# Differential attention: scores of three maps in one PSUM tile of five banks, queries split once, norms for two heads at a time

## The chip, the core and the metric

The kernel runs on one core of a Trainium2 chip. TensorE (PE, with its weight loads PEld) multiplies, VectorE (DVE), ScalarE (ACT) and GpSimd (POOL) do the rest, and SyncE (SP) issues the transfers. Sums of matmuls land in PSUM, which has eight banks of 512 float32 columns in each of 128 partitions. The metric is the device time of one execution in microseconds (us).

## What is computed

Two layers of a backbone over 512 latent tokens and 256 context tokens, 1024 wide. In each layer a modulated norm feeds one input projection, whose columns go to a gated MLP over chunks, to a differential attention and to a convolution module; one output projection (`w_out`) and a gated residual follow, and then a gated feed-forward part. The change is in the attention:

```
def diff_attn(q, k, v, lam):
    s = jnp.einsum("bqhmd,bkhmd->bhmqk", q, k) * (B_QK_DIM ** -0.5)
    p = jax.nn.softmax(s, axis=-1)
    a = p[:, :, 0] - lam * p[:, :, 1]
    return jnp.einsum("bhqk,bkhd->bqhd", a, v)
...
o = blocked_diff_attn(q, k_all, v_all, lam)        # 4 heads, 2 softmax maps per head
yb = rms_norm(o, P["subln_g"]) * (1.0 - lam_init)  # norm over the 128 columns of a head
```

Latent queries see 768 keys (512 latent, 256 context); context queries see the 256 context keys, in layer 0 only.

## The kernel before

**Units.** Queries are taken in pairs of tiles: `pairs` lists (head, p) with p = 0, 1 for two halves of the latent tokens and p = 2 for the context, which comes first and in layer 0 alone. So layer 0 has 12 pairs and layer 1 has 8. Each pair is two units of 128 queries, and each unit has two maps. I call the units of a pair A and B, and their maps a0, a1, b0, b1. Over both layers there are 64 maps of 768 keys and 16 of 256 keys.

**A unit.** `scores` (L801 to L819) does for each map: matmuls of the high part (L812) and the low part (L813) of the queries with the keys `kk` into `pss`, the negated maximum over the keys on VectorE (`mx`, L815), and the exp on ScalarE (`e`), which reads `pss` again and sums into `sm`. `combine` (L820 to L833) makes the factor `cc` on VectorE, adds the two maps into one (`e`, L831) and keeps a diagonal tile `dg` on POOL, for the norm's small term. `transp` transposes the result in blocks of 128 keys on TensorE (`pat`, L113) and copies it to `ath`. `attn_v` (L853) multiplies with the values (`po`, L860), a float32 matmul in two passes, for both units of a pair; `subln` (L868) does the norm with a matmul against ones (`pr`), Ln and Exp, and splits the result into `yBh` and `yBl`.

**Queries.** `q_prep` (L776) transposes a pair's queries (`pq`). For the first pair of a layer ScalarE copies the high part to `qh`, twice, since a map's 64 rows are wanted in both halves of the partitions; for the others it goes through `qn`, with copies by ScalarE and POOL. VectorE subtracts for the low part into `qlz`, whose other half is zero.

**PSUM.** `pss` has two buffers of two banks, tag "w" (`pq`, `pat`, `po`, `pr`) three buffers of one bank, tag "f" one bank.

**Fill.** A part of the output projection, which needs no attention result (`wout` with part 0, tile `wo`, tag "f"), is written out behind the unit loop (L906 to L911): two slices in layer 0, three in layer 1. In layer 0 one group of it stands ahead of the loop.

**Order.** The text of the loop is not the order on the engines. A list scheduler sets it from priorities and from when buffers come free, with `scores` and `q_prep` a little ahead (SCP), and each engine then works through its own list, waiting on semaphores. A tile is what the scheduler tracks: it places a wait on the engine that last used the tile's buffer.

Of the kernel before, what the change touches and what calls it, by code (L numbers as in the profile page):

```python
# [9 lines left out]
F32 = mybir.dt.float32  # L10
F32R = mybir.dt.float32r
# [5 lines left out]
P = 128  # L17
# [27 lines left out]

FB, WB, EB, QB = 1, 3, 5, 3
MRB, MRW, RAWB, NSQ, NTB, KXB, FTB = 4, 2, 3, 2, 3, 3, 2

HP, SCP, RSP = 1000, 2, 60
# [29 lines left out]
def tile_backbone(  # L81
# [27 lines left out]
    def sub_lo(o, a, hi, eng=None):  # L109
        (eng or V).tensor_sub(o, a, hi.bitcast(F32))  # L110
# [211 lines left out]
    for l in range(DEPTH):  # L322
# [433 lines left out]
        with ExitStack() as ph:  # L756
# [5 lines left out]
            qlz = [sp.tile([P, 2, 256], F32R, name=f"qlz{x}") for x in range(2)]  # L762
            zero = sp.tile([P, 256], F32, name="zero")
            G.memset(zero, 0.0)
            for x in qlz:
                for m in range(2):
                    ms = slice((1 - m) * QKD, (2 - m) * QKD)
                    G.tensor_copy(x[ms, m], zero[ms])
            pairs = [(h, p) for p in range(2) for h in range(HEADS)]
            if not last:  # L770
                pairs = [(h, 2) for h in range(HEADS)] + pairs
            units = [(n, i) for n in range(len(pairs)) for i in range(2)]
            st = {}

            def q_prep(n):
                h, p = pairs[n]  # L776
                qh = sp.tile([P, 2, 256], F32R, tag="qh", name="qh", bufs=QB)
                ql = qlz[n % 2]
                pq = ps.tile([P, 256], F32, tag="w", name="pq", bufs=WB)
                for i in range(2):  # L780
                    T.transpose(pq[:, i * P:(i + 1) * P], qt[2 * p + i][:, h * P:(h + 1) * P], ident)
                if n == 0:
                    for m in range(2):
                        for a in range(2):
                            S.copy(qh[a * QKD:(a + 1) * QKD, m], pq[m * QKD:(m + 1) * QKD])
                    for m in range(2):
                        ms = slice(m * QKD, (m + 1) * QKD)
                        sub_lo(ql[ms, m], pq[ms], qh[ms, m])
                else:
                    qn = sp.tile([P, 256], F32R, tag="qn", name="qn", bufs=2)  # L790
                    S.copy(qn, pq)
                    for m in range(2):
                        src = qn[m * QKD:(m + 1) * QKD]
                        for a in range(2):
                            (G.tensor_copy if a else S.copy)(qh[a * QKD:(a + 1) * QKD, m], src)
                    for m in range(2):
                        ms = slice(m * QKD, (m + 1) * QKD)
                        sub_lo(ql[ms, m], pq[ms], qn[ms])
                st["q", n] = (qh, ql)

            def scores(n, i):  # L801
                h, p = pairs[n]
                k0, nk = (0, 6) if p < 2 else (LAT, 2)
                qh, ql = st["q", n]
                e = []
                sm = sp.tile([P, 2], F32, tag="sm", name="sm", bufs=4)
                for m in range(2):
                    pss = ps.tile([P, 1024], F32, tag="s", name="pss", bufs=2)
                    for (a, b) in ([(0, 512), (512, 768)] if p < 2 else [(0, 256)]):
                        ksl = slice(k0 + a, k0 + b)  # L810
                        qs = slice(i * P, (i + 1) * P)
                        T.matmul(pss[:, a:b], qh[:, m, qs], kk[:, 2 * h + m, ksl], start=True, stop=False)  # L812
                        T.matmul(pss[:, a:b], ql[:, m, qs], kk[:, 2 * h + m, ksl], start=False, stop=True)  # L813
                    mx = sp.tile([P, 1], F32, tag="mx", name="mx", bufs=4)
                    V.tensor_reduce(out=mx, in_=pss[:, :nk * P], op=ALU.max, axis=AX.X, negate=True)  # L815
                    em = sp.tile([P, TOK], F32, tag="e", name="e", bufs=EB)
                    act(em[:, :nk * P], pss[:, :nk * P], AF.Exp, bias=mx, accum_out=sm[:, m:m + 1])
                    e.append(em)
                st[n, i] = (e, sm)  # L819

            def combine(n, i):
                nk = 6 if pairs[n][1] < 2 else 2
                e, sm = st[n, i]
                cc = sp.tile([P, 1], F32, tag="cc", name="cc", bufs=4)
                if i == 0:
                    st["dg", n] = sp.tile([P, 2, P], F32, tag="dg", name="dg", bufs=3)
                dg = st["dg", n][:, i]
                V.reciprocal(out=cc, in_=sm[:, 1:2])
                V.scalar_tensor_tensor(out=cc, in0=cc, scalar=nlam, in1=sm[:, 0:1], op0=ALU.mult, op1=ALU.mult)
                e0, e1 = e[0][:, :nk * P], e[1][:, :nk * P]  # L830
                V.scalar_tensor_tensor(out=e0, in0=e1, scalar=cc, in1=e0, op0=ALU.mult, op1=ALU.add)  # L831
                G.tensor_scalar(out=dg, in0=epsi, scalar1=sm[:, 0:1], scalar2=sm[:, 0:1], op0=ALU.mult, op1=ALU.mult)
                st[n, i] = e[0]  # L833

            def transp(n, i):
                nk = 6 if pairs[n][1] < 2 else 2
                e = st[n, i]
                if i == 0:
# [12 lines left out]

            def attn_v(n):
                h, p = pairs[n]  # L853
                k0, nk = (0, 6) if p < 2 else (LAT, 2)
                at = st[n]
                po = ps.tile([P, 256], F32, tag="w", name="po", bufs=WB)
                hs = slice(h * P, (h + 1) * P)
                for c in range(nk):
                    kt = k0 // P + c
                    T.matmul(po, vt[:, kt, hs], at[:, c], start=c == 0, stop=c == nk - 1)  # L860
                o = sp.tile([P, 256], F32, tag="o", name="o", bufs=2)
                sq = sp.tile([P, 256], F32, tag="osq", name="osq", bufs=2)
                S.copy(o, po)
                S.activation(sq, o, AF.Square)
                G.tensor_add(sq, sq, st["dg", n].rearrange("p a q -> p (a q)"))
                st["sub", n] = (o, sq)

            def subln(n):  # L868
                h, p = pairs[n]
                o, sq = st["sub", n]  # L870
# [5 lines left out]
                ts = slice(p * 256, p * 256 + 256)  # L876
                S.copy(yBh[:, h, ts], o)
                sub_lo(yBl[:, h, ts], o, yBh[:, h, ts])

            first = [(g, i) for g in whole for i in range(2)]  # L880
            if l == 0:
                w0 = wout_w(0, (0,), "pool")
                g, i = first.pop(0)
                wout(0, (0,), w0, [g], ps, "f", FB, (i,))
            q_prep(0)
            nu = len(units)
            for u in range(nu + 8):
# [12 lines left out]
                if 0 <= v < nu and units[v][1] == 1:  # L900
                    attn_v(units[v][0])
                v = u - LAG[2]
                if 0 <= v < nu and units[v][1] == 1:
                    subln(units[v][0])

            for mp2 in range(NFILL[l]):  # L906
                if mp2 == 0 and l == 0:
                    for g, i in first:
                        wout(0, (0,), w0, [g], ps, "f", FB, (i,))
                else:  # L910
                    wout(mp2, (0,), wout_w(mp2, (0,), "pool"), whole, ps, "f", FB)  # L911
        kvs.close()


# [253 lines left out]
```

## Time and profile before

| | before |
|---|---|
| three runs | 1617.92, 1620.43, 1620.6 us, median 1620.43 |
| the profiled execution, its own time | 1616.07 us |
| span in the trace | 1614.0 us |
| TensorE busy | 1570.6 us (97%) |
| VectorE, ScalarE, POOL busy | 1020.4, 646.9, 105.9 us |
| mean granted clock of TensorE | 0.994 |

The span is the time from the first to the last recorded instruction of the profiled execution. Busy times are sums over each engine; TensorE's is modelled, since its matmuls overlap. Start times below are us from the span's start, and clock 1.00 is TensorE's level of 2.4 GHz.

### The profile page before, as it was taken

The numbers are of one execution on the slowest core, as the hardware profiler recorded it, in microseconds if no ns is written. First come the engines' busy times: TensorE is split into PE (matmuls) and PEld (weight loads), VectorE is DVE, ScalarE is ACT, GpSimd is POOL, SyncE is SP. The second block draws the span as 40 slices with busy tenths as digits, with TensorE's granted clock in tenths as the row PEclk, the third lists the DMA queues.
The fourth block names the chain that finished last, engine by engine and source line by source line (L and its number), as shares of the span: only waits on it lengthen the run. The fifth ranks groups of instructions, "written<-read, shape, count | busy, mean of one in ns | idle before, by whom it ended". The sixth has DMA issues, their size and how long they took to land.

```text
span 1614.0 us, 21207 instructions
## 1 busy us (share of the span) xinstructions
PE 1570.6 (97%) x8186; PEld 1292.4 (80%) x8186; DVE 1020.4 (63%) x1722; ACT 646.9 (40%) x1122; POOL 105.9 (7%) x126
## 2 busy tenths in 40 slices
PE   6999998999999999999999999999999999999999
PEld 4875776778888887878888887887778788888888
DVE  4497878969999983345544244896976544334433
ACT  5431568753532322234433133254764333123321
POOL 1130125310000000000000000000220000000000
PEclk9999999999999999999999999999999999999999
DMA  7625110015255888988611235653022322332232
GB/s 282 212 76 180 56 64 15 14 51 185 85 190 194 285 279 265 289 284 298 207 66 50 60 127 186 205 170 105 27 80 78 104 92 88 95 104 92 92 105 92
DMA packets 83140, 222.93 MB, mean 138 GB/s; under 512 B 12256, under 2 KB 14560, under 8 KB 82912
## 3 DMA queue, kind: packets, MB, share of 16 engines
q1 hardware_dynamic: 83040, 221.59, 41.6%
q8 instruction: 64, 1.05, 0.3%
q14 instruction: 36, 0.29, 0.1%
HBM read 190.10 MB, written 31.46 MB: 137 GB/s over the span
## 4 chain that ended last, share of the span: by engine, by line
PE 77%; DMA 10%; DVE 6%; ACT 4%; issue 2%; SPq 0%; POOL 0%; POOLq 0%; DVEq 0%; ACTq 0%
PE pp L267 10%; PE pp L266 10%; PE pp L268 10%; PE acc L433 5%; PE acc L441 5%; PE acc L434 5%; PE pd L268 4%; PE pd L267 4%; PE pd L266 4%; DMA in<-araw 3%; DMA araw<-in_w_in_dram 3%; PE po L860 3%; PE wo L266 2%; DMA mraw<-in_w_modT_dram 2%; PE wo L267 2%; PE wo L268 2%
## 5 line engine op out<-in xcount | busy, mean ns | idle before, releaser
L268 PE MATMUL pp<-hhi,wlo 128*128 128x512 f32 (+1 forms) x1072 | 380.0, 355 | 4.4 <-DVE wlo L110 4.4
L266 PE MATMUL pp<-hhi,whi 128*128 128x512 f32 (+1 forms) x1072 | 380.6, 356 | 1.7 <-ACT whi L224 1.4
L267 PE MATMUL pp<-hlo,whi 128*128 128x512 f32 (+1 forms) x1072 | 381.4, 356 | 0.8 <-DVE hlo L306 0.8
L224 ACT CAST whi<-raw 128x1024 fp32r<-128x1024 f32 (+1 forms) x167 | 170.9, 1025 | 389.9 <-PE pp L267 203.0
L110 DVE TENSOR_TENSOR wlo<-raw,whi 128x1024 fp32r<-128x1024 f32 (+2 forms) x154 | 185.4, 1206 | 218.4 <-ACT whi L224 211.1
L268 PEld LDWEIGHTS pp<-hhi,wlo 128*128 128x128 f32 x1072 | 202.3, 189 | 36.1 <-DVE wlo L110 5.2
L266 PEld LDWEIGHTS pp<-hhi,whi 128*128 128x128 f32 x1072 | 202.0, 189 | 36.0 <-ACT whi L224 3.3
L267 PEld LDWEIGHTS pp<-hlo,whi 128*128 128x128 f32 x1072 | 202.0, 189 | 32.8 <-DVE hlo L306 1.5
L266 PE MATMUL pd<-gh,whi 128*128 128x512 f32 (+1 forms) x550 | 192.9, 351 | 2.5 <-ACT whi L224 2.5
L268 PE MATMUL pd<-gh,wlo 128*128 128x512 f32 (+1 forms) x550 | 193.6, 352 | 0.8 <-DVE wlo L110 0.8
L267 PE MATMUL pd<-gl,whi 128*128 128x512 f32 (+1 forms) x550 | 193.1, 351 | 0.0
L266 PEld LDWEIGHTS pd<-gh,whi 128*128 128x128 f32 x550 | 103.8, 189 | 18.0 <-ACT whi L224 2.9
L268 PEld LDWEIGHTS pd<-gh,wlo 128*128 128x128 f32 x550 | 104.1, 189 | 15.7 <-DVE wlo L110 1.0
L267 PEld LDWEIGHTS pd<-gl,whi 128*128 128x128 f32 x550 | 103.9, 189 | 15.1
L691 DVE SCALAR_TENSOR_TENSOR cacc<-cin,cw,cacc 128x783 f32<-128x783 f32 (+1 forms) x120 | 103.4, 916 | 3.4 <-ACT cacc L686 3.4
L110 DVE TENSOR_TENSOR araw<-araw,ahi 128x512 f32<-128x512 f32 x56 | 38.5, 691 | 93.3 <-ACT ahi L248 93.2
L1027 DVE TENSOR_TENSOR ft<-ft,pp 128x256 f32<-128x256 f32 (+1 forms) x66 | 39.1, 598 | 74.4 <-PE pp L268 66.7
L196 DVE CUSTOM_DVE_ANT_0 mraw<-mraw,csil,bmod 128x1024 f32<-128x1024 f32 x64 | 81.7, 1279 | 5.9 <-DMA mraw<-in_w_modT_dram 5.5
L248 ACT CAST ahi<-araw 128x512 fp32r<-128x512 f32 x56 | 34.7, 620 | 121.5 <-DMA araw<-in_w_in_dram 83.7
L433 PE MATMUL acc<-whi,hhi 128*128 128x512 f32 x192 | 77.8, 405 | 0.0
L434 PE MATMUL acc<-whi,hlo 128*128 128x512 f32 x192 | 76.9, 401 | 0.0
L101 ACT ACTIVATE ft<-ft 128x768 f32<-128x768 f32 (+1 forms) x44 | 32.6, 740 | 103.2 <-DVE ft L1022 103.2
(224 smaller groups left out, 2599.3 us busy)
## 6 DMA issues: line engine op xcount, KB each, us to landing
raw<-in_w_gv_dram SPq DMA_DIRECT2D x88, 512.0 KB, 3.3
mraw<-in_w_modT_dram SPq DMA_DIRECT2D x64, 512.0 KB, 4.3
raw<-in_w_down_dram SPq DMA_DIRECT2D x34, 512.0 KB, 3.6
wh<-in SPq DMA_DIRECT2D x24, 512.0 KB, 4.4
wl<-in SPq DMA_DIRECT2D x24, 512.0 KB, 4.5
raw<-in_w_in_dram SPq DMA_DIRECT2D x20, 512.0 KB, 4.1
araw<-in_w_in_dram SPq DMA_DIRECT2D x40, 256.0 KB, 3.6
in<-ahi SPq DMA_DIRECT2D x40, 256.0 KB, 4.7
```

What stands on the lines that cost most here:

```text
L110: (eng or V).tensor_sub(o, a, hi.bitcast(F32))
L196: r = V.tensor_tensor_reduce(out=junk, in0=w, in1=csil[:, s], scale=1.0, scalar=bmod[:, l, i, f:f + 1], op0=ALU.mult, op1=ALU.add, accum_o ...
L224: S.copy(hi, raw)
L266: T.matmul(o, lhi, rhi, start=start, stop=False)
L267: T.matmul(o, lhi, rlo, start=False, stop=False)
L268: T.matmul(o, llo, rhi, start=False, stop=stop)
L433: T.matmul(pt[t], hhi[hs], wh[:, a], start=k2 + a == 0, stop=False)
L434: T.matmul(pt[t], hlo[hs], wh[:, a], start=False, stop=False)
L441: T.matmul(pt[t], hhi[hs], wl[:, a], start=False, stop=k2 + 1 == KD // 2 and a == 1)
L691: V.scalar_tensor_tensor(out=cacc[:, c, :cn], in0=cin[:, c, j:j + cn], scalar=cw[:, l, c, j:j + 1], in1=cacc[:, c, :cn], op0=ALU.mult, op1 ...
L860: T.matmul(po, vt[:, kt, hs], at[:, c], start=c == 0, stop=c == nk - 1)
L1027: V.tensor_mul(t[:, a:b], t[:, a:b], pp[s][1][:, :b - a])
```

## The change

All maps go into one tile `sbank` of five banks. The map with the number nmap takes the 768 columns that start at 0, 768 or 1536 in turn; its matmuls are cut where a bank ends. The tag "f" is gone: the fill uses tag "w", as `pq`, `pat`, `po` and `pr` do. The queries are split once into `qn` (high and low part, 128 rows each), and four transfers on SP's queue (64x2x256 values each) put them into both halves of `qq`. The norm handles two heads: one Square, one Ln, one Exp and one write of `yBh` and `yBl` for two, and the term `dg` comes in by a matmul of its own (L862) in place of an addition on POOL. In `transp` the second copy of unit B moves from VectorE to ScalarE, and `dg` has five buffers.

```diff
-FB, WB, EB, QB = 1, 3, 5, 3
+WB, EB, QB = 3, 5, 3
...
+            sbank = ps.tile([P, 5 * 512], F32, name="sbank")
+            nmap = [0]
...
-                qh = sp.tile([P, 2, 256], F32R, tag="qh", name="qh", bufs=QB)
-                ql = qlz[n % 2]
+                qq = sp.tile([P, 2, 2, 256], F32R, tag="qq", name="qq", bufs=QB)
+                qn = sp.tile([P, 2, 256], F32R, tag="qn", name="qn", bufs=2)
                 pq = ps.tile([P, 256], F32, tag="w", name="pq", bufs=WB)
...
-                    S.copy(qn, pq)
-                    for m in range(2):
-                        src = qn[m * QKD:(m + 1) * QKD]
-                        for a in range(2):
-                            (G.tensor_copy if a else S.copy)(qh[a * QKD:(a + 1) * QKD, m], src)
-                    for m in range(2):
-                        ms = slice(m * QKD, (m + 1) * QKD)
-                        sub_lo(ql[ms, m], pq[ms], qn[ms])
-                st["q", n] = (qh, ql)
+                S.copy(qn[:, 0], pq)
+                sub_lo(qn[:, 1], pq, qn[:, 0])
+                for m in range(2):
+                    for a in range(2):
+                        nc.sync.dma_start(out=qq[a * QKD:(a + 1) * QKD, :, m].bitcast(F32), in_=qn[m * QKD:(m + 1) * QKD].bitcast(F32))
+                st["q", n] = (qq[:, 0], qq[:, 1])
...
-                    pss = ps.tile([P, 1024], F32, tag="s", name="pss", bufs=2)
-                    for (a, b) in ([(0, 512), (512, 768)] if p < 2 else [(0, 256)]):
+                    x0 = nmap[0] % 3 * TOK
+                    nmap[0] += 1
+                    pss = sbank[:, x0:x0 + TOK]
+                    cut = 256 if x0 % 512 else 512
+                    for (a, b) in ([(0, cut), (cut, TOK)] if p < 2 else [(0, 256)]):
...
-                    if c0 == 0:
+                    if c0 == 0 or i == 1:
                         S.copy(at[osl], pat[:, :cn_])
...
-                G.tensor_add(sq, sq, st["dg", n].rearrange("p a q -> p (a q)"))
...
-                pr = ps.tile([P, 256], F32, tag="w", name="pr", bufs=WB)
-                T.matmul(pr, ones, sq, start=True, stop=True)
+                pr = ps.tile([P, 2, 256], F32, tag="w", name="pr", bufs=WB)
+                for y in range(2):
+                    T.matmul(pr[:, y], ones, sq[:, y], start=True, stop=False)
+                    T.matmul(pr[:, y], ones, st["dg", 2 * x + y].rearrange("p a q -> p (a q)"), start=False, stop=True)
...
-                wout(0, (0,), w0, [g], ps, "f", FB, (i,))
+                wout(0, (0,), w0, [g], ps, "w", WB, (i,))
...
-                if 0 <= v < nu and units[v][1] == 1:
-                    subln(units[v][0])
+                if 0 <= v < nu and units[v][1] == 1 and units[v][0] % 2 == 1:
+                    subln(units[v][0] // 2)
```

How this stands on the engines is shown at three places. First TensorE in layer 1, before, where a pair is well under way: two maps have a tile `pss` each, `pat` of another unit and the fill `wo` stand between their matmuls.

```order
L113 MATMUL pat_10001<-ident_62,e_9922 128x128 [waits DVE_49]
L812 MATMUL pss_9985<-kk_9207,qh_9902 128x512 [waits Activation_49,Pool_49]
L113 MATMUL pat_10001<-ident_62,e_9922 128x128
L813 MATMUL pss_9985<-kk_9207,qlz1_9885 128x512
L113 MATMUL pat_10001<-ident_62,e_9922 128x128
L812 MATMUL pss_9985<-kk_9207,qh_9902 128x256
L113 MATMUL pat_10001<-ident_62,e_9922 128x128
L813 MATMUL pss_9985<-kk_9207,qlz1_9885 128x256
L113 MATMUL pat_10007<-ident_62,e_9922 128x128 x2
L266 MATMUL wo_10716<-yACh_8637,wh_10698 128x512
L267 MATMUL wo_10716<-yACl_8638,wh_10698 128x512
L268 MATMUL wo_10716<-yACh_8637,wl_10700 128x512
```

The same part of the program after: all maps write `sbank`, `pat` and `po` stand between two maps, and no `wo` is there.

```order
L113 MATMUL pat_9945<-ident_62,e_9851 128x128 [waits DVE_49,PE_49]
L113 MATMUL pat_9945<-ident_62,e_9851 128x128 x3
L113 MATMUL pat_9951<-ident_62,e_9851 128x128 [waits PE_49]
L113 MATMUL pat_9951<-ident_62,e_9851 128x128
L848 MATMUL po_9955<-ath_9867,vt_9089 128x256 [waits PE_49]
L848 MATMUL po_9955<-ath_9867,vt_9089 128x256 x3
L800 MATMUL sbank_9765<-kk_9088,qq_9777 128x256 [waits Activation_49]
L801 MATMUL sbank_9765<-kk_9088,qq_9777 128x256
L800 MATMUL sbank_9765<-kk_9088,qq_9777 128x512
L801 MATMUL sbank_9765<-kk_9088,qq_9777 128x512
L848 MATMUL po_9955<-ath_9867,vt_9089 128x256 x2
L800 MATMUL sbank_9765<-kk_9088,qq_9833 128x512 [waits DMAHW7_49,DMAHW6_49,Activation_49]
```

The transposes, which trailed the maps by several, stand right behind one map each, and the fill has left this place.

Second, ScalarE in layer 1 before: `e` are the exps of the maps, in the order of the maps.

```order
L101 ACTIVATE e_9947,sm_9939<-pss_9940,mx_9945 128x768
L101 ACTIVATE e_9956,sm_9939<-pss_9949,mx_9954 128x768
L101 ACTIVATE e_9983,sm_9975<-pss_9976,mx_9981 128x768
L848 COPY ath_10000<-pat_10001 128x4x128
L101 ACTIVATE e_9992,sm_9975<-pss_9985,mx_9990 128x768
L848 COPY ath_10000<-pat_10035 128x4x128
L101 ACTIVATE e_10019,sm_10011<-pss_10012,mx_10017 128x768
L101 ACTIVATE e_10028,sm_10011<-pss_10021,mx_10026 128x768
L791 CAST qn_10049<-pq_10046 128x256
```

And after, over one pair:

```order
L101 ACTIVATE e_9859,sm_9844<-sbank_9765,mx_9857 128x768
L836 COPY ath_9944<-pat_9945 128x4x128
L101 ACTIVATE e_9885,sm_9878<-sbank_9765,mx_9883 128x768
L851 COPY o_9962<-po_9955 128x256
L101 ACTIVATE e_9893,sm_9878<-sbank_9765,mx_9891 128x768
L836 COPY ath_9944<-pat_9986 128x4x128
L101 ACTIVATE e_9928,sm_9921<-sbank_9765,mx_9926 128x768
L836 COPY ath_9944<-pat_9992 128x2x128
L779 CAST qn_9997<-pq_9998 128x256
L101 ACTIVATE e_9936,sm_9921<-sbank_9765,mx_9934 128x768
```

Two exps that stood together are now parted by copies of `ath`, `o` and `qn`, which wait for TensorE.

Third, TensorE at the end of layer 1's attention before: `pr` are the sums of the norms, `wo` the fill.

```order
L860 MATMUL po<-ath,vt 128x256 x6
L872 MATMUL pr<-osq,ones 128x256
L113 MATMUL pat<-ident,e 128x128 x6
L266 MATMUL wo<-yACh,wh 128x512
L267 MATMUL wo<-yACl,wh 128x512
L268 MATMUL wo<-yACh,wl 128x512
L860 MATMUL po<-ath,vt 128x256 x6
L872 MATMUL pr<-osq,ones 128x256
L266 MATMUL wo<-yACh,wh 128x512
L267 MATMUL wo<-yACl,wh 128x512
L268 MATMUL wo<-yACh,wl 128x512
L266 MATMUL wo<-yACh,wh 128x512
```

And after:

```order
L113 MATMUL pat<-ident,e 128x128 x6
L848 MATMUL po<-ath,vt 128x256 x6
L861 MATMUL pr<-osq,ones 128x256
L862 MATMUL pr<-dg,ones 128x256
L861 MATMUL pr<-osq,ones 128x256
L862 MATMUL pr<-dg,ones 128x256
L266 MATMUL wo<-yACh,wh 128x512
L267 MATMUL wo<-yACl,wh 128x512
L268 MATMUL wo<-yACh,wl 128x512
```

All of the fill of this layer stands behind the last `pr`; layer 0 reads likewise.

## Rows read from the trace of the kernel before

**Rows 1.** Timeline of TensorE, first and next matmul of both stages: start, us, instruction

```profile
244.22 0.82 PE L781 MATMUL pq<-ident,q 128*128 128x128 f32 x6
...
349.49 0.58 PE L267 MATMUL wo<-yACl,whi 128*128 128x512 f32 x1
...
1121.80 0.81 PE L781 MATMUL pq<-ident,q 128*128 128x128 f32 x6
...
1123.01 0.50 PE L812 MATMUL pss<-kk,qh 128*128 128x512 f32 x1
...
1204.68 0.58 PE L267 MATMUL wo<-yACl,wh 128*128 128x512 f32 x1
```

**Rows 2.** Windows 245-300, 300-349, 1123-1160, 1160-1205: their sum, busy us by engine

```profile
sum 186.00, PE 172.34 PEld 140.12 DVE 159.83 ACT 139.72 POOL 60.14; mean PE 43.08 PEld 35.03 DVE 39.96 ACT 34.93 POOL 15.04
```

**Rows 3.** Waits, 245 to 349: us in total, times, longest us

```profile
PE pss L812 <- ACT e L101: 6.3, 9, 1.1
```

**Rows 4.** Timeline of all engines, 277 to 281 us

```profile
277.27 0.85 PE L113 MATMUL pat<-ident,e 128*128 128x128 f32 x6 [0.24 <-ACT osq L101]
...
277.94 0.58 ACT L848 COPY ath<-pat 128x512 f32<-128x512 f32 x1 [0.73 <-PE pat L113]
...
278.42 0.91 ACT L101 ACTIVATE e<-pss,mx 128x768 f32<-128x768 f32 x1
...
279.45 0.16 DVE L828 RECIPROCAL cc<-sm 128x1 f32<-128x1 f32 x1 [0.19 <-ACT e L101]
...
279.47 0.50 PE L812 MATMUL pss<-kk,qh 128*128 128x512 f32 x1 [1.13 <-ACT e L101]
...
279.60 0.38 ACT L791 CAST qn<-pq 128x256 fp32r<-128x256 f32 x1
...
279.98 0.42 DVE L110 TENSOR_TENSOR yBl<-o,yBh 128x256 fp32r<-128x256 f32 x1
...
280.16 0.28 PE L813 MATMUL pss<-kk,qlz 128*128 128x256 f32 x1
```

**Rows 5.** Timeline, layer 1, scores and the maximum behind them

```profile
1144.20 0.28 PE L813 MATMUL pss<-kk,qlz 128*128 128x256 f32 x1
...
1144.52 0.96 DVE L815 TENSOR_REDUCE mx<-pss 128x1 f32<-128x768 f32 x1 [0.27 <-PE pss L813]
```

**Rows 6.** Timeline, layer 0, a map of 256 keys

```profile
248.47 0.39 PE L812 MATMUL pss<-kk,qh 128*128 128x256 f32 x1 [0.79 <-ACT e L101]
...
248.69 0.28 PE L813 MATMUL pss<-kk,qlz 128*128 128x256 f32 x1
...
249.15 0.42 DVE L815 TENSOR_REDUCE mx<-pss 128x1 f32<-128x256 f32 x1
...
249.61 0.47 ACT L101 ACTIVATE e<-pss,mx 128x256 f32<-128x256 f32 x1 [0.32 <-DVE mx L815]
```

**Rows 7.** Groups by line and shape, 1123 to 1205: busy us, mean ns

```profile
L831 DVE SCALAR_TENSOR_TENSOR e<-e,cc 128x768 f32<-128x768 f32 x16 | 16.2, 1010 | 0.1
```

**Rows 8.** Timeline of TensorE, layers 0 and 1

```profile
340.00 2.86 PE L860 MATMUL po<-ath,vt 128*128 128x256 f32 x12
...
1146.14 0.39 PE L267 MATMUL wo<-yACl,wh 128*128 128x512 f32 x1
1146.37 0.40 PE L268 MATMUL wo<-yACh,wl 128*128 128x512 f32 x1
```

**Rows 9.** Windows: length, busy by engine, granted clock, DMA share, GB/s

```profile
248.00:250.00 2.00, 0.96 (x4) 0.59 (x4) 1.88 (x8) 1.66 (x7) 1.44 (x4) 1.00 0.08 33
252.00:254.00 2.00, 2.00 (x8) 1.61 (x8) 1.63 (x7) 0.76 (x3) 0.44 (x1) 0.50 0.00 0
276.00:280.00 4.00, 2.62 (x16) 2.06 (x15) 3.81 (x9) 3.23 (x9) 1.54 (x2) 1.00 0.00 0
```

**Rows 10.** DMA issues: count, KB each, median us to landing

```profile
out_dram<-xT SPq DMA_DIRECT2D x4, 128.0 KB, 1.8
...
gbase<-in_qk_g_dram SPq DMA_DIRECT2D x2, 128.0 KB, 3.7
```

More of the change, by code (lines that the diff above doesn't have):

```diff
@@ L760, in tile_backbone @@
             V.tensor_scalar_mul(gsub, sublt[:, l:l + 1], 1.0 - lam0)
[L762 to L765, printed above, removed]
-                for m in range(2):
-                    ms = slice((1 - m) * QKD, (2 - m) * QKD)
-                    G.tensor_copy(x[ms, m], zero[ms])
             pairs = [(h, p) for p in range(2) for h in range(HEADS)]
@@ L781, in q_prep @@
                     T.transpose(pq[:, i * P:(i + 1) * P], qt[2 * p + i][:, h * P:(h + 1) * P], ident)
-                if n == 0:
-                    for m in range(2):
-                        for a in range(2):
-                            S.copy(qh[a * QKD:(a + 1) * QKD, m], pq[m * QKD:(m + 1) * QKD])
-                    for m in range(2):
-                        ms = slice(m * QKD, (m + 1) * QKD)
-                        sub_lo(ql[ms, m], pq[ms], qh[ms, m])
-                else:
-                    qn = sp.tile([P, 256], F32R, tag="qn", name="qn", bufs=2)
-                    S.copy(qn, pq)
-                    for m in range(2):
-                        src = qn[m * QKD:(m + 1) * QKD]
-                        for a in range(2):
-                            (G.tensor_copy if a else S.copy)(qh[a * QKD:(a + 1) * QKD, m], src)
-                    for m in range(2):
-                        ms = slice(m * QKD, (m + 1) * QKD)
-                        sub_lo(ql[ms, m], pq[ms], qn[ms])
-                st["q", n] = (qh, ql)
+                S.copy(qn[:, 0], pq)
[4 more added lines that the diff above has]
+                st["q", n] = (qq[:, 0], qq[:, 1])
             def scores(n, i):
@@ L825, in combine @@
                 if i == 0:
-                    st["dg", n] = sp.tile([P, 2, P], F32, tag="dg", name="dg", bufs=3)
+                    st["dg", n] = sp.tile([P, 2, P], F32, tag="dg", name="dg", bufs=5)
                 dg = st["dg", n][:, i]
@@ L860, in attn_v, with subln @@
                     T.matmul(po, vt[:, kt, hs], at[:, c], start=c == 0, stop=c == nk - 1)
-                o = sp.tile([P, 256], F32, tag="o", name="o", bufs=2)
-                sq = sp.tile([P, 256], F32, tag="osq", name="osq", bufs=2)
-                S.copy(o, po)
-                S.activation(sq, o, AF.Square)
-                G.tensor_add(sq, sq, st["dg", n].rearrange("p a q -> p (a q)"))
[L866 to L870, printed above, removed]
-                pr = ps.tile([P, 256], F32, tag="w", name="pr", bufs=WB)
-                T.matmul(pr, ones, sq, start=True, stop=True)
+                if n % 2 == 0:
+                    st["sub", n // 2] = sp.tile([P, 2, 256], F32, tag="o", name="o", bufs=2)
+                S.copy(st["sub", n // 2][:, n % 2], po)
+            def subln(x):
+                h, p = pairs[2 * x]
+                o = st["sub", x]
+                sq = sp.tile([P, 2, 256], F32, tag="osq", name="osq", bufs=2)
+                S.activation(sq, o, AF.Square)
+                pr = ps.tile([P, 2, 256], F32, tag="w", name="pr", bufs=WB)
+                for y in range(2):
+                    T.matmul(pr[:, y], ones, sq[:, y], start=True, stop=False)
+                    T.matmul(pr[:, y], ones, st["dg", 2 * x + y].rearrange("p a q -> p (a q)"), start=False, stop=True)
                 act(sq, pr, AF.Ln, scale=1.0 / P)
@@ L875, in subln @@
                 V.scalar_tensor_tensor(out=o, in0=o, scalar=gsub, in1=sq, op0=ALU.mult, op1=ALU.mult)
-                ts = slice(p * 256, p * 256 + 256)
-                S.copy(yBh[:, h, ts], o)
-                sub_lo(yBl[:, h, ts], o, yBh[:, h, ts])
+                osl = (slice(None), slice(h, h + 2), slice(p * 256, p * 256 + 256))
+                S.copy(yBh[osl], o)
+                sub_lo(yBl[osl], o, yBh[osl])
             first = [(g, i) for g in whole for i in range(2)]
@@ L908, in tile_backbone @@
                     for g, i in first:
-                        wout(0, (0,), w0, [g], ps, "f", FB, (i,))
+                        wout(0, (0,), w0, [g], ps, "w", WB, (i,))
                 else:
-                    wout(mp2, (0,), wout_w(mp2, (0,), "pool"), whole, ps, "f", FB)
+                    wout(mp2, (0,), wout_w(mp2, (0,), "pool"), whole, ps, "w", WB)
         kvs.close()
```

## Prediction

> **What bounds the kernel now.** I read the page first, then the busy time of the attention stages by windows, then the waits there, then the timeline around single maps. Attention runs twice. In layer 0 TensorE starts it with `pq` at 244.22, and the matmul behind the last `pr` starts at 349.49; in layer 1 the same two stand at 1121.80 and 1204.68 [rows 1]. In these stretches TensorE is busy for 172.3 of 186.0 us, VectorE 159.8, ScalarE 139.7 [rows 2]. The reader is to see three engines that are nearly full at once: TensorE has the end, and 13.7 us is all that its idle time could give back. Its wait for ScalarE's exp `e` is 6.3 us in nine places [rows 3]: with two buffers a map waits for the exp of the map two before, which is mostly over. What keeps TensorE full is that the `wout` fill, `pat` and `po` stand between the maps.
>
> **The new order of maps.** The two listings of TensorE show what the program text hides. `sbank` is one tile, and the first matmul of each map waits for ScalarE; counted through ScalarE's order, the count it asks for is that of the exp of the map directly ahead, whichever columns that one read. So there is not a depth of three but of one: scores, maximum, exp, and only then the next scores.
>
> One link, from single rows. Exp ends at 278.42+0.91 = 279.33 and the scores start at 279.47: 0.14. They end at 280.16+0.28: 0.97 for four matmuls [rows 4]. From their end to the maximum is 1144.52-1144.48 = 0.04, the maximum takes 0.96 [rows 5]; in the 256-key map it ends at 249.57 and the exp starts at 249.61: 0.04 [rows 6]. The exp takes 0.91 [rows 4]. Together 3.03 us for a map of 768 keys. For 256 keys: 0.14, scores 248.47 to 248.97 = 0.50, 0.04, 0.42, 0.04, 0.47 [rows 6], together 1.61. There are 64 large maps (8 pairs x 4 in each layer) and 16 small ones: 64x3.03 + 16x1.61 = 219.7 us of bare chain, while both stages now take 105.3 + 82.9 with everything in them. This alone puts the kernel behind.
>
> **What else stands in the chain.** The listings of TensorE and ScalarE put other work into it. A walk through one large pair, from the end of the exp of its map a1 at 0: next scores 0.14 to 1.11. VectorE meanwhile has reciprocal (0.12 after the exp's end, 0.16 long [rows 4]), `cc` and the long combination (start at 0.58, 1.01 long [rows 7]); it stands before the maximum of b0, which so runs 1.59 to 2.54. `pat` starts behind the combination at 1.70, its first copy 0.67 later, 0.58 long [rows 4], and that copy stands before exp(b0): 2.95 to 3.85 in place of 2.13 to 3.03. Four `po` matmuls stand before the scores of b1: each is two passes, and twelve passes last 2.86, the last some 0.4 of it [rows 8], so 0.22 each: eight take 1.75 and end at 4.15, 0.16 after the exp's hand-over; `po` again 0.88, the copy `o` before exp(b1), which ends at 7.42. The second half goes likewise, with `qn` (0.38) and the low half (0.42) [rows 4] before the last maximum: the pair ends at 14.4, and with `pr` on TensorE in every second pair 14.5. Bare chain: 12.1. The same walk with the small rows gives 8.2 for a small pair (bare 6.4).
>
> **Clock.** TensorE would be busy some 60% of this. At 0.96 of 2 us in 248 to 250 the granted clock was still full, and in 252 to 254 it was 0.50 (1.2 GHz); at 2.62 of 4 in 276 to 280 it was 1.00 [rows 9]. The large pairs lie near the latter, the small ones near the former. At the 1.2 GHz level the scores of a pair cost 3.9 more (2.0 for small maps): 18.4 and 10.2. I take a fifth of that way for the large pairs, 15.3, and half of it for the small, 9.2; the ends stay for the range.
> The Trainium skill's page "TensorE: Matmul & The Clock Gate", section "A second HAM failure mode: psum-queue depth-cycling", says that short idle times between groups of matmuls can make the clock go back and forth between its levels. By that rule the sum would be that of the second rival; the row at 276 to 280 speaks against it at the large maps, the one at 252 to 254 for it.
>
> **Fill.** It now takes tag `w` and stands behind the last `pr` in both layers. A 512-wide matmul starts 0.23 after the last [rows 8], a 256-wide one at half. Layer 0: 48 wide and 36 narrow = 15.4, of which all but 1.8 lie inside the stage now; layer 1: 72 wide = 16.7, all but 1.2 inside. In before they cover waits; now nothing runs beside them but the end of the norms.
>
> **Start.** `pq` to first scores is 1123.01-1121.80 = 1.2 now [rows 1]. After: `pq` 0.25, `qn` 0.38, low half 0.42, then DMAs. Their landing is not in the trace for this size from SBUF; the nearest rows, 128 KB each, land in 1.8 and 3.7 [rows 10]. With two issues ahead and hand-overs, 3.6 to 5.8; I take 4.8, and no fill stands beside it. For later pairs `pq` stands some five maps (15 us) ahead, which hides the DMAs; without that cover each pair would pay about 4.
>
> **End.** Behind the last exp: combination to 1.6, `pat` and copies to 3.0, `po` 2.6, copy, Square and four `pr` 2.8 and hand-overs, 8.7; less 0.9 that the walk counts already: 7.8.
>
> **At nothing.** Fewer qh copies, one low half in place of two, no zeroing, no POOL sum, norms of two heads in one instruction, one copy moved to ScalarE: VectorE, ScalarE and POOL then wait for the chain, so what is saved lies in their idle time. `dg` in `pr` adds 40 passes of some 0.22 [rows 8], 8.8 us of TensorE, covered by the exps; if the cover were gone, 8.8 is its price. SP's queue has the q DMAs behind weight loads that are early.
>
> **Sum.** Layer 0: 4.8 + 4x9.2 + 8x15.3 + 7.8 + 15.4 = 187.2. Layer 1: 4.8 + 122.4 + 7.8 + 16.7 = 151.7. Together 338.9. Before: 105.3+1.8 and 82.9+1.2 = 191.2. More by 147.7: on the profiled execution's 1616.1 it makes 1763.8. The median of the runs, 1620.4, lies 4.4 above that execution: **1768**.
>
> **Rivals.**
> 1. *The bare chain.* Everything but scores, maximum and exp fits into gaps: 219.7 + 2x(4.8+7.8) + 32.1 = 277.0, more by 85.8: 1706. For it: much of the walk's extra is hand-over that I estimated. Against: ScalarE's order has the copies before the exps.
> 2. *The 1.2 GHz level throughout.* 4x10.2 + 16x18.4 + 25.2 + 32.1 = 392.5, more by 201.3: 1822. For it the row of 252 to 254, against it that of 276 to 280.
> 3. *Other side: maps wait by bank.* If a map waited only for readers of its own banks, two maps in a row wait for each other (they share a bank) and the third is free: three maps in two links, 2.02 us per map, against some 2.6 now (82.9 us for 32 maps). The chain would not bind; the 13.7 us of idle could go and 8.8 of `dg` come: 4.9 less, 1616. It decides for faster as long as the uncovered start costs less than 4.9 us in all; if start and end are uncovered twice, it turns to about +20 (1640). Against it: the counts of the waits, which are those of the map ahead for free columns too.
> The Trainium skill's page "PSUM — Partial Sum Buffer", section "PSUM bank collisions raise a hardware error", has the rule to guard by bank and quadrant, not by address; by it, this third case would be allowed. No row of the kernel before has one tile over five banks, so none shows how it is guarded.
>
> **Numbers.** The forecast 0.62; rival 1 0.13; rival 2 0.15; rival 3 on the slow side 0.06; rival 3 faster 0.02, and its two effects cancelling 0.02. Between the bare chain and the low clock lies nine tenths: 1706 to 1822. A measurement tells about 0.2% from no change: faster 0.02, same 0.02, slower 0.96.
>
> **What would show it.** Right: in both attention stages TensorE's largest wait is `sbank` for `e`, once per map, starts of maps lie 3.0 to 4.5 us apart; the stages last near 170 and 135 us without the fill; `wo` runs alone behind `pr`; VectorE's time per map is unchanged. The clock there tells the forecast from rival 2, and the time between an exp's end and the maximum of the next map tells it from rival 1. Wrong: scores that run beside the exp of the map ahead.

## The result, and the profile after

| | before | after |
|---|---|---|
| median of the runs | 1619.37 us (1617.92 to 1620.6, 4 runs) | 1768.67 us (1766.87 to 1772.21, 4 runs) |
| profiled execution, its span | 1614.0 us | 1770.4 us |
| mean granted clock | 0.994 | 0.954 |

The ratio is 1.0927, 95% interval 1.091 to 1.0944: slower by 9.3%, 149.3 us. The forecast was 1768, with 1706 to 1822.

The page of the changed kernel, first the busy times, then TensorE's busy tenths and granted clock in 40 slices of 44 us:

```profile
PE 1632.5 (92%) x8226; PEld 1335.2 (75%) x8226; DVE 1011.7 (57%) x1666; ACT 633.9 (36%) x1056; POOL 62.8 (4%) x60
...
PE   7999976768999999998999999996669999999998
...
PEclk8999986889999999999999999996889999999999
```

The same two rows of the kernel before:

```profile
PE   6999998999999999999999999999999999999999
PEclk9999999999999999999999999999999999999999
```

After, there are two dents, slices 6 to 10 (in the clock row 6 to 9) and 28 to 30. They lie in the two attention stages; elsewhere the rows differ from those of before by a tenth in single slices.

The stages' ends on TensorE, from the timeline of the changed kernel:

```profile
244.23 1.18 PE L778 MATMUL pq<-ident,q 128*128 128x128 f32 x6
250.18 0.55 PE L800 MATMUL sbank<-kk,qq 128*128 128x256 f32 x1 [4.76 <-DMA qq<-qn]
...
415.66 0.59 PE L862 MATMUL pr<-dg,ones 128*128 128x256 f32 x2
...
1205.04 0.82 PE L778 MATMUL pq<-ident,q 128*128 128x128 f32 x6
...
1210.12 0.77 PE L800 MATMUL sbank<-kk,qq 128*128 128x512 f32 x1 [4.26 <-DMA qq<-qn]
...
1344.05 0.59 PE L862 MATMUL pr<-dg,ones 128*128 128x256 f32 x2
```

From `pq` to the end of the last `pr` layer 0 takes 172.0 us and layer 1 139.6. Read the same way, before takes 105.6 and 83.2 (the 105.3 and 82.9 of [rows 1] end where the matmul behind the last `pr` starts), with nearly all of the fill inside; after, none of it is inside. The waits of the changed kernel over the whole span (us in total, times, longest):

```profile
DVE mx L803 <- PE sbank L801: 85.1, 55, 5.2
PE sbank L800 <- ACT e L101: 74.1, 48, 2.5
```

The wait for exp was 6.3 us before, over the whole span too, all of it in layer 0 [rows 3]; now it is 74.1, at 48 of the 80 maps. And the maximum waits for the scores, 55 times: each engine waits for the one ahead in the chain. One half of a large pair in layer 1, with the exp of map a1 first:

```profile
1248.65 0.90 ACT L101 ACTIVATE e<-sbank,mx 128x768 f32<-128x768 f32 x1 [1.58 <-DVE mx L803]
...
1249.69 0.58 PE L800 MATMUL sbank<-kk,qq 128*128 128x256 f32 x1 [2.13 <-ACT e L101]
...
1250.12 1.02 DVE L819 SCALAR_TENSOR_TENSOR e<-e,cc 128x768 f32<-128x768 f32 x1
...
1250.71 0.63 PE L801 MATMUL sbank<-kk,qq 128*128 128x512 f32 x1
1251.38 0.96 DVE L803 TENSOR_REDUCE mx<-sbank 128x1 f32<-128x768 f32 x1 [0.24 <-PE sbank L801]
...
1252.41 0.58 ACT L836 COPY ath<-pat 128x512 f32<-128x512 f32 x1 [2.77 <-PE pat L113]
1252.60 1.95 PE L848 MATMUL po<-ath,vt 128*128 128x256 f32 x8
...
1252.89 0.91 ACT L101 ACTIVATE e<-sbank,mx 128x768 f32<-128x768 f32 x1
...
1254.19 0.59 PE L800 MATMUL sbank<-kk,qq 128*128 128x512 f32 x1
...
1255.35 0.96 DVE L803 TENSOR_REDUCE mx<-sbank 128x1 f32<-128x768 f32 x1 [2.09 <-PE sbank L801]
1256.15 0.37 ACT L851 COPY o<-po 128x256 f32<-128x256 f32 x1 [2.26 <-PE po L848]
1256.41 0.91 ACT L101 ACTIVATE e<-sbank,mx 128x768 f32<-128x768 f32 x1
...
1257.46 0.50 PE L800 MATMUL sbank<-kk,qq 128*128 128x512 f32 x1 [1.35 <-ACT e L101]
...
1257.90 1.02 DVE L819 SCALAR_TENSOR_TENSOR e<-e,cc 128x768 f32<-128x768 f32 x1
...
1258.15 0.28 PE L801 MATMUL sbank<-kk,qq 128*128 128x256 f32 x1
1258.84 0.95 DVE L803 TENSOR_REDUCE mx<-sbank 128x1 f32<-128x768 f32 x1
```

The scores of b0 start at 1249.69, 0.14 after the exp's end, though they write other columns than that exp read. The copy `ath` (1252.41) stands ahead of exp(b0) at 1252.89; `po`, from 1252.60, stands ahead of the scores of b1 at 1254.19; the copy `o` ahead of exp(b1). These are the walk's steps in its order, but for one: here it is not the combination (1250.12 to 1251.14) that holds the maximum of b0 back. The scores themselves end only at 1251.34, after 1.65 us in place of 0.97, and the maximum starts 0.04 later; over 1249.6 to 1251.4 the granted clock was 0.50, the 1.2 GHz level. In the next half the scores take 0.97 (1257.46 to 1258.43, with a clock of 0.93 over 1257.4 to 1259.9), and there the combination, 1257.90 to 1258.92, does hold the maximum back.

For comparison, the next map in layer 1 before, behind the scores that end at 1144.48 [rows 5]:

```profile
1144.35 0.48 PE L812 MATMUL pss<-kk,qh 128*128 128x512 f32 x1
...
1146.03 0.91 ACT L101 ACTIVATE e<-pss,mx 128x768 f32<-128x768 f32 x1
```

Its scores start 1.7 us ahead of the exp of the map before it.

### The profile page after: what moved, and what is told of

It is laid out like the page before. It is cut to its first block, busy times and chain, and to the rows that moved or that the text cites. A ratio compares the mean times of both kernels' runs of the same rounds, so it can differ in the third digit from the quotient of the medians.

```text
span 1770.4 us, 21260 instructions
## 1 busy us (share of the span) xinstructions
PE 1632.5 (92%) x8226; PEld 1335.2 (75%) x8226; DVE 1011.7 (57%) x1666; ACT 633.9 (36%) x1056; POOL 62.8 (4%) x60
## 4 chain that ended last, share of the span: by engine, by line
PE 46%; DMA 7%; ACT 2%; DVE 2%; issue 1%; SPq 0%; ACTq 0%; DVEq 0%
PE pp L267 6%; PE pp L268 6%; PE pp L266 6%; PE pd L268 4%; PE pd L267 4%; PE pd L266 4%; PE acc L433 2%; PE acc L441 2%; PE acc L434 2%; DMA in<-araw 2%; DMA araw<-in_w_in_dram 2%; DMA araw<-in_w_out_dram 2%; PE po L848 1%; ACT e L101 1%; PE sbank L800 1%; PE pat L113 1%
## 5 line engine op out<-in xcount | busy, mean ns | idle before, releaser
L800 PE MATMUL sbank<-kk,qq 128*128 128x256 f32 (+1 forms) x144 | 70.3, 492 | 83.1 <-ACT e L101 74.1
L803 DVE TENSOR_REDUCE mx<-sbank 128x1 f32<-128x768 f32 (+1 forms) x80 | 68.0, 850 | 85.4 <-PE sbank L801 85.1
L800 PEld LDWEIGHTS sbank<-kk,qq 128*128 128x128 f32 x144 | 34.6, 240 | 103.1 <-ACT e L101 90.2
L101 ACT ACTIVATE e<-sbank,mx 128x768 f32<-128x768 f32 (+1 forms) x80 | 65.5, 818 | 51.5 <-DVE mx L803 51.0
```

Of the source, the lines that this page charges most:

```text
L101: r = S.activation(out, in_, func, **kw)
```

## Experiments

All times of a row are medians; the ratio is against the kernel before on the same chip, with its 95% interval. "Stages" are from `pq` to the end of the last `pr`, layer 0 and layer 1, read from each timeline. The fill is either inside or behind them (32 us). "2 of 3 wait" means that of three maps in a row two share a tile and wait for each other. Stages and all other rows of a trace are from one execution; only the medians are from several.

| kernel | maps in flight | fill | us | ratio | stages |
|---|---|---|---|---|---|
| before | 2 | inside | 1618.3 to 1625.4 | 1 | 105.6, 83.2 |
| after | 1 | behind | 1768.67 | 1.0927 (1.091 to 1.0944) | 172.0, 139.6 |
| e1_two_tiles | 2 of 3 wait | behind | 1673.41 | 1.0345 (1.0324 to 1.0365) | 120.4, 97.6 |
| e2_fill_own_bank | 1 | inside | 1722.04 | 1.0645 (1.0624 to 1.0667) | 168.1, 133.6 |
| e3_before_one_tile | 1 | inside | 1719.47 | 1.0629 (1.0605 to 1.0654) | 166.3, 129.9 |
| e4_pairs_of_banks | 2 | inside | 1617.92 | 1.0005 (0.9993 to 1.0017) | 111.4, 85.1 |
| e5_fill_in_w | 2 | behind | 1654.49 | 1.0191 (1.0114 to 1.0269) | 107.4, 87.2 |
| e6_w_two_banks | 1 | behind | 1771.72 | 1.0914 (1.0838 to 1.099) | 171.0, 135.7 |
| e7_idle_filled | 1 | behind | 1745.64 | 1.0753 (1.0694 to 1.0812) | 158.9, 126.6 |
| e8_three_pairs | 3 | behind | 1649.77 | 1.0162 (1.0099 to 1.0226) | 106.2, 82.0 |
| e9_two_tiles_fill | 2 of 3 wait | inside | 1640.16 | 1.013 (1.0098 to 1.0162) | 117.1, 96.7 |
| e10_sum_on_pool | 2 | inside | 1617.65 | 0.9991 (0.9975 to 1.0007) | 109.5, 82.8 |
| e11_first_pair_direct | 2 | inside | 1609.88 | 0.9941 (0.9919 to 0.9964) | 102.6, 79.7 |
| e12_one_added | 2 | behind | 1647.72 | 1.0177 (1.0143 to 1.0211) | 105.0, 83.7 |

The median of before was 1618.3 beside e1 to e4, 1625.4 (three runs) beside e5 to e8 and 1618.8 beside e9 to e12.

### Is it the shared tile?

**e1_two_tiles** divides the same five banks at a bank's edge:

```diff
-            sbank = ps.tile([P, 5 * 512], F32, name="sbank")
+            sbank = ps.tile([P, 3 * 512], F32, name="sbank")
+            sbank2 = ps.tile([P, 2 * 512], F32, name="sbank2")
...
-                    pss = sbank[:, x0:x0 + TOK]
+                    pss = sbank[:, x0:x0 + TOK] if x0 < 2 * TOK else sbank2[:, :TOK]
```

> The changed kernel with its five banks as two tiles: the slots at 0 and 768 in one of three banks, the third slot in one of two banks; all else as changed, the fill behind the last pr included. Theory (a map waits for the exp of the map ahead because all maps share one tile): of three maps only the pair in the shared tile waits for each other, so a large pair falls from about 16 us to 10 to 11.5 and the time from 1769 to 1660 to 1695. Rival (the uncovered fill, start and end and the low clock are most of the loss, whatever the maps wait for): the pairs shorten by less than 2 us each and the time stays above 1735.

**e3_before_one_tile** goes the other way, from the kernel before:

```diff
+            sbank = ps.tile([P, 2048], F32, name="sbank")
...
-                    pss = ps.tile([P, 1024], F32, tag="s", name="pss", bufs=2)
+                    x0 = nmap[0] % 2 * 1024
+                    nmap[0] += 1
+                    pss = sbank[:, x0:x0 + 1024]
```

> The kernel before with one edit: the two buffers of scores are two halves of one tile of four banks; queries, norms and the fill's own bank as before. Theory: this edit alone makes one map in flight and costs most of the 149 us of the change less the fill, start and end: 1690 to 1725. Rival (the loss comes from the fill, the q transfers and the order): within 1% of before, 1620 to 1636.

The theory has both. The division takes 95.3 us off the changed kernel, and one tile puts 101.1 on the kernel before. In e3 nothing but the tile differs, so the shared tile alone makes some 101 of the 149.3 us. The wait of TensorE for exp in e3, and in e1, over the whole span:

```profile
PE sbank L816 <- ACT e L101: 51.1, 35, 2.1
```

```profile
PE sbank L801 <- ACT e L101: 23.5, 25, 2.1
```

In e3 the two halves of the tile share no bank, and the scores wait for the other half's exp all the same. One such place in layer 1 of e3, where the exp ends at 1228.67 and the scores into the other half start 0.15 later, TensorE having stood idle for 2.08 us until then:

```profile
1227.77 0.90 ACT L101 ACTIVATE e<-sbank,mx 128x768 f32<-128x768 f32 x1 [0.63 <-DVE mx L819]
...
1228.82 0.50 PE L816 MATMUL sbank<-kk,qh 128*128 128x512 f32 x1 [2.08 <-ACT e L101]
```

### Is it the fill?

**e2_fill_own_bank** (its diff follows; tag "w" gives up a bank for the fill), and the fill moved the other way round on the kernel before, **e5_fill_in_w** ("w" keeps its three banks):

```diff
-WB, EB, QB = 3, 5, 3
+FB, WB, EB, QB = 1, 2, 5, 3
...
-                    wout(mp2, (0,), wout_w(mp2, (0,), "pool"), whole, ps, "w", WB)
+                    wout(mp2, (0,), wout_w(mp2, (0,), "pool"), whole, ps, "f", FB)
```

> The changed kernel with sbank as it is, but the fill in a tag of its own with one bank and tag w with two banks. Theory: one map in flight stays, the fill moves into the waits; its 29 us behind the last pr go, and the clock rises with TensorE's share, so 1710 to 1740, with sbank for e still the largest wait of TensorE. Rival (the place of the fill is the main cost): below 1680. If the fill delays the scores instead: 1745 or more.

> The kernel before with one edit: the fill uses tag w in place of its own bank, so it stands behind the last pr of each layer; two separate tiles for scores as before. Theory (the place of the fill costs what it uncovers): with two maps in flight the other engines still need most of the stage, so the 32 us of fill come behind it and the stage without it gets shorter by some 10 to 20 us: 1628 to 1645. Rival (the place of the fill costs the 47 us that lie between e2_fill_own_bank and the changed kernel, with or without the shared tile): 1660 or more.

With the shared tile the fill's place is worth 46.6 us (1768.67 to 1722.04), as the theory had it; that "w" has two banks plays no part, as e6 shows below (1771.72). The wait for exp falls by half, since `wo` fills it, and the pace of the maps nearly stays, 15.2 and 15.0 us for a large pair in place of 15.5 and 15.7:

```profile
PE sbank L800 <- ACT e L101: 37.1, 30, 2.2
```

With two tiles the same edit costs 29.1 us against the kernel before on its chip (1625.4). The expectation missed: it gave 8 to 25 us over a before of 1620, and the rival 40 or more. The interval is wide, 18 to 44 us, and reaches into both; the times alone do not part them, and the traces must. The stages get no shorter (107.4 and 87.2 against 105.6 and 83.2), so the fill costs what it uncovers and the stage gives nothing back. Busy time by engine (PE, PEld, DVE, ACT, POOL), then the granted clock, in the stages of before, first layer 0:

```profile
245.40:349.50 104.10, 93.82 (x502) 76.47 (x500) 90.31 (x188) 80.80 (x212) 36.83 (x63) 0.97 0.03 11
1123.00:1204.70 81.70, 78.17 (x413) 63.33 (x412) 69.98 (x130) 58.55 (x139) 22.99 (x41) 1.00 0.14 46
```

and in those of e5:

```profile
245.70:351.80 106.10, 85.10 (x428) 68.16 (x427) 84.94 (x181) 79.28 (x211) 37.45 (x63) 0.94 0.05 16
1146.20:1232.00 85.80, 71.37 (x347) 58.06 (x347) 67.45 (x125) 59.33 (x139) 22.24 (x41) 0.90 0.09 31
```

TensorE has 15.5 us less to do in the two stages, yet they are longer, at a granted clock of 0.94 and 0.90 in place of 0.97 and 1.00. **e12_one_added** asks whether that clock is the cause:

```diff
...
+                    T.matmul(dum, kk[:, 0, :P], kk[:, 0, :512], start=True, stop=True)
                     mx = sp.tile([P, 1], F32, tag="mx", name="mx", bufs=4)
...
```

> e5_fill_in_w with one added matmul of 512 columns for each map in the bank that the fill left, 80 in all, 18.6 us of TensorE, whose result nothing reads. The stages of e5 are as long without the fill as they are with it before. If the clock is what keeps them long (0.90 and 0.93 there): the granted clock goes to about 1.00 and the stages get shorter by 3 to 8 us in spite of the added work. If the chain of maximum and exp in two buffers keeps them long: the same within 2 us. If TensorE were the bound: longer by 10 or more.

```profile
245.70:349.30 103.60, 91.25 (x475) 72.47 (x474) 84.89 (x181) 78.67 (x211) 35.32 (x63) 0.98 0.05 16
1142.30:1223.90 81.60, 71.87 (x378) 58.54 (x376) 67.40 (x125) 58.84 (x138) 21.88 (x40) 0.98 0.09 31
```

With the added work the clock is at 0.98 and the stages are shorter by 2.5 and 3.5 us than in e5. These are single executions on two chips, and the times do not bear the gain out: over before on its own chip e12 costs 28.9 us and e5 29.1, with overlapping intervals. So that the clock is part of it is suggested and not shown. What e12 does show is that the added matmuls, 18.6 us of TensorE by the expectation, make the stages no longer (105.0 and 83.7), so TensorE's work does not set its length. What does, two maps in flight with the maximum and the exp in turn perhaps, was not taken apart further.

### What does the clock cost?

**e6_w_two_banks** is the control (`WB` 2 in place of 3), **e7_idle_filled** adds matmuls for each map, in the bank set free:

```diff
...
+                    for _ in range(5 if p < 2 else 3):
+                        T.matmul(dum, kk[:, 0, :P], kk[:, 0, :512], start=True, stop=True)
```

> Control for e7_idle_filled: the changed kernel with two banks in place of three for tag w, nothing else. A third bank frees room only for work that waits for the chain of maps anyway: 1760 to 1785.

> As e6_w_two_banks, with added matmuls of the keys with themselves, whose result nothing reads, five of 512 columns for each large map and three for each small one, in the bank that e6 freed. They do no work for the output and fill TensorE's idle time. Theory (in the forecast the clock takes some 17 us over both stages, and in the trace it was at its lower level for about a third of the stages): the granted clock there goes to 1.00 and the time falls by 10 to 35 us below e6. Rival (the lower clock lies in waits and costs nothing): same as e6 or longer by what the added matmuls delay.

The stages of e6 from the first scores on (PE, PEld, DVE, ACT, POOL, clock):

```profile
250.80:415.50 164.70, 117.96 (x451) 87.03 (x451) 78.94 (x148) 72.03 (x171) 10.74 (x24) 0.75 0.17 42
1210.50:1340.90 130.40, 94.33 (x363) 69.24 (x364) 62.27 (x100) 53.16 (x115) 7.16 (x16) 0.76 0.18 45
```

and of e7:

```profile
250.10:403.00 152.90, 136.74 (x640) 103.21 (x641) 78.58 (x148) 71.34 (x171) 10.74 (x24) 0.93 0.19 46
1197.40:1318.60 121.20, 108.54 (x506) 81.25 (x507) 61.65 (x100) 53.16 (x115) 7.16 (x16) 0.94 0.19 49
```

VectorE and ScalarE do the same work in both. The clock goes from 0.75 and 0.76 to 0.93 and 0.94 and, on the same chip, the time falls by 26.1 us, 21.3 of it in the stages, though TensorE is busy for 33 us more. In the changed kernel itself the clock goes back and forth, in stretches of 4 us:

```profile
364.00:368.00 4.00, 1.44 (x9) 0.77 (x7) 1.52 (x3) 2.42 (x6) 0.45 (x1) 1.00 0.03 7
368.00:372.00 4.00, 3.36 (x12) 2.86 (x13) 2.57 (x5) 1.22 (x4) 0.00 (x0) 0.58 0.55 124
372.00:376.00 4.00, 4.00 (x21) 3.53 (x20) 1.18 (x2) 1.56 (x4) 0.45 (x1) 0.99 0.01 2
376.00:380.00 4.00, 2.54 (x15) 1.78 (x13) 2.93 (x5) 2.91 (x6) 0.00 (x0) 1.00 0.01 4
380.00:384.00 4.00, 1.43 (x5) 1.15 (x6) 1.98 (x5) 2.12 (x6) 0.45 (x1) 0.79 0.00 0
```

### Queries, norms and more maps in flight

**e4_pairs_of_banks** has the bank plan of before, with queries and norms as changed:

```diff
...
-                    pss = sbank[:, x0:x0 + TOK]
+                    pss = ps.tile([P, 1024], F32, tag="s", name="pss", bufs=2)
...
```

> The changed kernel with the PSUM plan of before: two tiles of two banks for scores, three banks for tag w, one for the fill; queries split once with q transfers and norms for two heads as changed. Theory: near before, 1615 to 1640, the start of each layer some 3 us later at most. Rival (q transfers or the two-head norms cost much of the change): above 1660.

It is the kernel before to 0.2%. The whole 9%, taken net, is the bank plan. **e8_three_pairs** gives three maps tiles of their own (`bufs=3`, `WB` 2, the fill in "w"), and **e9_two_tiles_fill** joins e1 and e2:

> The changed kernel with three separate tiles of two banks each for the scores and two banks for tag w, which the fill shares; queries and norms as changed. Each map then waits for the exp of the map three before. Theory: the chain no longer binds, what stays is the fill behind the last pr and the uncovered start and end: 1630 to 1655. Rival (the number of banks in tag w or the order of pat and po sets the pace): above 1680.

> Both remedies at once in the five banks of the change: two tiles as in e1_two_tiles, and the fill in a bank of its own with two banks for tag w as in e2_fill_own_bank. Theory (shared tile and uncovered fill are the two causes): 1620 to 1645. If a third cause of the size of 30 us or more is left in the order of the maps or in two banks for w: above 1650.

Both came out as expected. The stages of e8, with three maps in flight, are shorter than e5's by 1.2 and 5.2 us only, though e8's start is longer by 5.3 and 4.1; e8 has the queries and norms of the change, e5 those of before. **e10_sum_on_pool** takes the `dg` passes from TensorE again (the first piece below), **e11_first_pair_direct** also spares the first pair of a layer the transfers (the second):

```diff
-                    T.matmul(pr[:, y], ones, sq[:, y], start=True, stop=False)
-                    T.matmul(pr[:, y], ones, st["dg", 2 * x + y].rearrange("p a q -> p (a q)"), start=False, stop=True)
+                    G.tensor_add(sq[:, y], sq[:, y], st["dg", 2 * x + y].rearrange("p a q -> p (a q)"))
+                    T.matmul(pr[:, y], ones, sq[:, y], start=True, stop=True)
```

```diff
+                if n == 0:
+                    for m in range(2):
+                        for a in range(2):
+                            S.copy(qq[a * QKD:(a + 1) * QKD, 0, m], pq[m * QKD:(m + 1) * QKD])
+                    for m in range(2):
+                        for a in range(2):
+                            ms = slice(m * QKD, (m + 1) * QKD)
+                            sub_lo(qq[a * QKD:(a + 1) * QKD, 1, m], pq[ms], qq[ms, 0, m])
...
```

> e4_pairs_of_banks with the term dg added on POOL again, for each head, in place of 40 passes in TensorE; norms still for two heads, queries still split once. If the added passes cost their 8.8 us of TensorE: 1606 to 1613. If they lie in waits, or POOL's sum is late for pr: as e4, 1615 to 1622.

> e10_sum_on_pool with the first pair of each layer split straight from PSUM into both halves of its tile, without transfers (the other pairs as in e10). If the start of 5 to 6 us, which the fill covers there, still costs: 2 to 7 us below e10. If the fill covers it: within 2 us of e10.

e10 is the kernel before and e4 within what is measured: the passes cost nothing net. Whether they lay in waits, or what was saved went into POOL's sum, for which the last `pr` waits 2.0 us in layer 0 and 1.8 in layer 1 of e10, is open, as the expectation left it. e11 is faster than both kernels, by 0.6% of before, and 7.8 us below e10, a little more than expected: the first scores come 1.2 us after `pq` in place of 6.4 and 5.2, and that start had cost although the fill stood beside it.

## Why the prediction was right

**The chain.** That a map waits for the exp of the map ahead was read from the listing, and the trace shows it: 0.14 from exp to scores, the first link of the walk. (The terms of the bare link add up to 3.06, not 3.03; rival 1 becomes 2 us dearer by it.) e3 shows that it is the tile that does it, e1 that dividing the tile undoes it.

**The pair.** The forecast was 15.3 for a large pair; exp(a1) to exp(a1) of the next pair is 15.5 on the mean in layer 0 and 15.7 in layer 1 (14.9 to 16.2). At nearly full clock, in e7, most pairs take 13.7 to 14.0, against 14.5 by the walk: the steps were right in kind and order, and some 0.6 too dear in sum. At the lower clock one link is another than in the walk, as shown above: the scores and not the combination hold the maximum. A small pair was put at 9.2; the sixteen small exps lie 31.1 us apart from first to last, some 8.3 a pair.

**The clock.** The forecast took a fifth of the way to the 1.2 GHz level for the large pairs and half for the small, together some 17 us. e7 measures 21.3 in the stages, and its clock is still not full. The large pairs were nearer to the lower level than [rows 9] made me take them (granted clock 0.69 to 0.89 over three single pairs of layer 1), so the two errors, walk and clock, nearly cancelled; that is luck. The page "TensorE: Matmul & The Clock Gate" of the Trainium skill, section "A second HAM failure mode: psum-queue depth-cycling", says that short idle times between groups of matmuls can make the clock go back and forth; the trace agrees, with 0.58 to 1.00 in neighbouring stretches above. The prediction made the second rival of it, the lower level throughout; the page does not say that, and the mean clock of 0.77 in both stages does not show it:

```profile
244.23:416.25 172.02, 114.23 (x460) 88.62 (x459) 80.47 (x151) 72.61 (x173) 11.93 (x25) 0.77 0.19 46
1205.04:1344.64 139.60, 93.10 (x370) 71.96 (x369) 63.69 (x104) 54.14 (x118) 7.16 (x16) 0.77 0.19 50
```

**Start.** 4.8 was taken; it is 5.95 and 5.08. The landing is 2.4 us at the median, inside the 1.8 to 3.7 of [rows 10]. The term that was too small is the issue: two issues ahead were counted. In layer 0 the fourth transfer of the pair is issued at 247.89, and the scores start at 250.18, 2.29 later, which fits its landing (2.3 to 3.6 over all 80) and not that of the two that the first map reads; so three issues stand ahead. On SP's queue eight transfers take 5.74, some 0.7 each (0.61 at the median of all 80):

```profile
245.83 5.74 SPq L783 DMA_DIRECT2D qq<-qn  x8
```

**End.** 8.7 from the last exp to the end of the last `pr`; it is 9.0 in both layers.

**Fill.** 32.1 uncovered was the term; the edit is worth 46.6. The stages of e2 are shorter by 3.9 and 6.0 with the fill inside, which goes with a mean clock over the run of 0.970 in place of 0.954. The rest lies outside the stages: there e1, with the fill behind, takes 36.5 us longer than e2 on the same chip, 32.9 of it with TensorE busy and 3.6 idle. So this term was some 4.4 too small. The forecast had the clock in the pairs, not in the fill.

**At nothing.** Taken together, queries, norms and the `dg` passes are worth nothing that can be measured: e4 is the kernel before, and at one map in flight e2 and e3, on one chip, lie 2.6 us apart. With two maps in flight that is a balance and not nothing for each: e11 shows that the transfers of the first pairs cost 7.8, and without them the kernel is 8.9 faster than before, so the other edits give back about as much. Which of them does was not tested.

**The sum.** Stages and fill were put at 338.9; with the fill as put they are 172.0 + 139.6 + 32.1 = 343.7, 4.8 more. That 1768 was met to 0.7 us is in part luck: the sum gave 1763.8 for a profiled execution that took 1772.21, 8.4 too few. The 4.4 added for the median hid half of that, and that the profiled execution was 3.5 above its median nearly all of the rest.

**What failed.** "TensorE has the end" is the step that falls: e5 and e12 show that the stage of before does not get shorter when TensorE has less to do. It carried no term of the sum. In rival 3 the price was wrong: e1, whose tiles let just those maps wait that it describes, takes 1673, not 1616 to 1640, because the rival left out the fill, which is still behind there (33.2 us between e1 and e9), and its two links for three maps did not bring the pace of before. The Trainium skill's page "PSUM — Partial Sum Buffer", section "PSUM bank collisions raise a hardware error", has the rule to guard by bank and quadrant. What was built guards by tile: its two halves in e3 wait for each other without a bank in common.

**Open.** What e9 still lacks to before, 1.3%. Its later start, some 9 us over both layers, does not explain it, for e4 has that start too and lacks nothing. Its stages are 17.3 us longer than those of e4, from which it differs by the two maps that share a tile and by two banks for "w"; the two were not parted.

## What to carry to other kernels

Buffers are counted in tiles that are tracked apart, not in banks: one tile cut into three slots is one buffer, and the listing of waits shows it before anything runs. Filler work that has lost a buffer of its own moves behind the stage and costs its full time, some 29 us at two maps in flight here; at one map in flight it cost 46.6, and there the clock in the stages was 0.77 without it and 0.85 with it. Before calling an engine the bound because it is busy, ask what the stage would do without its filler.

## What was not expected of the hardware

Matmuls that do no work made the kernel faster, by 26.1 us at one map in flight (e7 against e6, on one chip), while the granted clock in the stages rose from 0.75 to 0.93. At two maps in flight it rose from 0.92 to 0.98 (e12 against e5), but no gain clear of noise came of it. A transfer of 128 KB from SBUF to SBUF landed in 2.4 us, but one queue took 0.6 to 0.7 us for each issue.
